# Gated encoder block on one core: the order of PSUM readings and attention-row sums around the gate products

## The chip, the cores and the metric

The kernel runs on one core of a Trainium2 chip. The metric is the device time of one execution in microseconds (us); the time before is the median of three runs. The engines are TensorE (PE in the profile; PEld is its loading of weights), VectorE (DVE), ScalarE (ACT), GpSimd (POOL) and SyncE (SP), which issues the transfers (DMA).

## What is computed

One residual layer over 1024 tokens of width 1024, in float32. Cut to what matters here:

```
h    = rms_norm(x)
proj = h @ w_in            # q, k, v of two attentions, and the gates g_a, g_b (1024 columns each)
o_a  = neighbourhood_attention(...)    # 1024 x 512
o_b  = sliding_window_attention(...)   # 1024 x 512
y    = sigmoid(g_a) * (o_a @ w_branch_a) + sigmoid(g_b) * (o_b @ w_branch_b)
x    = x + y @ w_out
x    = x + (silu(h2 @ w_gate) * (h2 @ w_up)) @ w_down      # h2 = rms_norm(x)
```

The change lies in the computation of g_a and g_b, and in the reading back of o_a and o_b, which the kernel has parked in DRAM.

## The kernel before

Every float32 operand is kept as two parts, hi (a cast, on ACT) and lo (the difference, on DVE). A product of a block is three matmuls of 128x512: hi by hi, hi by lo, lo by hi (L824 to L826).

The gates are computed in pairs. Pair d takes columns d of g_a and of g_b and both halves of the tokens, a product of 2 by 2 blocks, with seven block products instead of eight (class `Seven`, L788). Product p needs the weight g_p (hi and lo; some are sums s1 to s4 of weight blocks, made on DVE, L806), and one product is four blocks of three matmuls, twelve in all. The products of a pair run in the order (1, 5, 6, 2, 7, 3, 4) and add up in four PSUM banks named X, Y, V and Z; there are two such sets of banks, and pairs alternate between them. Pairs 2 and 3 are "early" (`early=d < 4`): they run in turn, product by product, in the order `EARLY` = (1, 2, 3, 5, 6, 7, 4), and there Z takes products 6, 7 and 4 on top of a copy of product 1. In the later pairs product 6 goes into Y, which begins as a copy of X, and ACT copies Y into Z (L828) before products 7 and 4 are added to it. The seventh pair is pair 7, the sixth pair 6.

A bank Z is read between products that go on adding to it: after product 6 in the early pairs (L889: Z plus the copy of V in `gp`), after product 7 (L893), and at the end (L875 in `out`). The next product into Z waits for such a reading. `out` (L874) multiplies a finished block by the row norms in `wide_rs` (into a tile `go`) and stores it in `g_dram`.

`load_o` (L919) reads back four rows (128 features each) of one attention output for one half of the tokens, each as two parts from `o_dram`; DVE adds the parts (L925, into one of two scratch tiles `os`), and `split` casts (ACT, L50) and subtracts (DVE, L51). Rows 4 to 7 belong to the sliding-window attention, rows 0 to 3 to the other. They are used after the gates, by the branch products (L427 to L429), which add into banks `pb`.

What sets the order: PE's is that of the program. SP's transfers made with `dma` (L95) keep the program's order too. On DVE and ACT a scheduler puts the instructions in order when the kernel is built, from its own estimate of times; `tc.issue_after(ins)` demands that what is made inside comes behind `ins` on that instruction's engine, and nothing else. Each engine then runs its queue in order. `prefetch(d + 2)`, behind product 2 in pairs 4 to 6, loads the weights of a later pair, or, from pair 6 on, the branch weights `wb` (`load_branch`, L931). Their casts and those of the next pair's weights are chained one behind the other (`in_chain`, L780).

## Time and profile before

| | |
|---|---|
| median of three runs | 1317.98 us (1316.93, 1317.98, 1318.95) |
| span of the profiled execution (first to last instruction) | 1314.8 us |
| what lies around the span, by the median | 3.2 us |
| mean granted TensorE clock | 1.000 |
| PE, DVE, ACT busy | 1304.5, 1018.5, 695.8 us |
| pairs 2 and 3 in the span | about 400.9 to 440.2 us |
| pairs 4 to 7 in the span | about 440.2 to 517.0 us |

The page shows the span of the profiled execution and no other time of it, so what lies around the span is taken from the median of the runs. Times in the timelines count from the span's start. A timeline row gives the start, the duration, the engine, the line, the operation, out<-in, the shapes, and in brackets the idle time of the engine before it and what ended that. Names are shown without buffer numbers, so `bankZ` stands for both banks Z and `go` for the tiles of all pairs. Lines are those of the kernel before.

### The profile page before, as it was taken

The numbers are of one execution on the slowest core, as the hardware profiler recorded it, in microseconds if no ns is written. First come the engines' busy times: TensorE is split into PE (matmuls) and PEld (weight loads), VectorE is DVE, ScalarE is ACT, GpSimd is POOL, SyncE is SP. The second block draws the span as 40 slices with busy tenths as digits, with TensorE's granted clock in tenths as the row PEclk, the third lists the DMA queues.
The fourth block names the chain that finished last, engine by engine and source line by source line (L and its number), as shares of the span: only waits on it lengthen the run. The fifth ranks groups of instructions, "written<-read, shape, count | busy, mean of one in ns | idle before, by whom it ended". The sixth has DMA issues, their size and how long they took to land.

```text
span 1314.8 us, 19624 instructions
## 1 busy us (share of the span) xinstructions
PE 1304.5 (99%) x6618; PEld 1133.6 (86%) x6618; DVE 1018.5 (77%) x2039; ACT 695.8 (53%) x1459; POOL 182.5 (14%) x322
## 2 busy tenths in 40 slices
PE   9999999999999999999999999999999999999998
PEld 8999999999888788888888888888888888888887
DVE  5678867776687758868999878888777799798774
ACT  6677857776664324636456544443444455363532
POOL 1364645564310000000000000000000000000000
PEclk9999999999999999999999999999999999999999
DMA  9532424252435348757774533233233356672532
GB/s 306 153 89 61 108 64 109 61 135 61 143 118 180 121 146 271 240 172 237 241 247 120 169 105 106 87 104 117 81 108 121 120 171 217 245 248 65 183 129 81
DMA packets 180997, 191.92 MB, mean 146 GB/s; under 512 B 21104, under 2 KB 126576, under 8 KB 180896
## 3 DMA queue, kind: packets, MB, share of 16 engines
q1 hardware_dynamic: 180640, 190.57, 46.5%
q8 instruction: 52, 0.85, 0.3%
q14 instruction: 49, 0.40, 0.1%
q10 hardware_dynamic: 256, 0.10, 0.0%
HBM read 133.19 MB, written 52.37 MB: 141 GB/s over the span
## 4 chain that ended last, share of the span: by engine, by line
PE 85%; DVE 6%; DMA 4%; ACT 2%; issue 1%; SPq 1%; POOL 1%; ACTq 0%; POOLq 0%; DVEq 0%
PE bankZ L824 6%; PE bankZ L825 5%; PE bankZ L826 5%; PE bankY L824 5%; PE bankY L826 5%; PE bankY L825 5%; PE pj L327 4%; PE bankX L824 4%; PE pj L326 4%; PE pj L325 4%; PE bankX L825 4%; PE bankX L826 4%; PE o L649 3%; PE bankV L825 3%; PE bankV L824 3%; PE bankV L826 3%
## 5 line engine op out<-in xcount | busy, mean ns | idle before, releaser
L603 ACT ACTIVATE E<-E,nm 128x384 f32<-128x384 f32 (+3 forms) x128 | 75.7, 592 | 48.3 <-DVE nm L597 42.4
L605 POOL TENSOR_SCALAR E<-E,nm 128x384 f32<-128x384 f32 (+1 forms) x128 | 74.3, 581 | 95.2 <-DVE nm L604 72.3
L51 DVE TENSOR_TENSOR pl<-tp,ph 128x384 fp32r<-128x384 f32 (+1 forms) x128 | 66.4, 519 | 17.2 <-ACT ph L50 16.2
L50 ACT CAST ph<-tp 128x384 fp32r<-128x384 f32 (+1 forms) x128 | 57.4, 449 | 20.5 <-PE tp L615 19.9
L50 ACT CAST f<-f 128x512 fp32r<-128x512 f32 x87 | 50.9, 620 | 22.2 <-DMA f<-u_dram 21.5
L51 DVE TENSOR_TENSOR f<-f 128x512 fp32r<-128x512 f32 x87 | 56.4, 684 | 8.0 <-ACT f L50 8.0
L615 PE MATMUL tp<-ident,E 128*128 128x128 f32 x352 | 59.5, 272 | 0.9 <-POOL E L605 0.9
L615 PEld LDWEIGHTS tp<-ident,E 128*128 128x128 f32 x352 | 45.2, 140 | 5.9 <-POOL E L605 1.2
L345 POOL TENSOR_TENSOR ss<-ss,mhalf 128x4 f32<-128x4 f32 (+2 forms) x42 | 49.7, 1184 | 3.2
L649 PE MATMUL o<-pl,v 128*128 128x256 f32 (+2 forms) x160 | 48.7, 305 | 0.6 <-DVE pl L51 0.5
L604 DVE RECIPROCAL nm<-nm 128x1 f32<-128x1 f32 x128 | 20.4, 160 | 36.1 <-ACT E L603 34.8
L1214 POOL TENSOR_TENSOR rs<-rs,mhalf 128x4 f32<-128x4 f32 x2 | 2.8, 1418 | 319.4 <-DVE rs L1213 319.4
L649 PE MATMUL o<-ph,v 128*128 128x256 f32 (+2 forms) x160 | 45.9, 301 | 0.5 <-ACT ph L50 0.5
L591 PE MATMUL s<-k,q 128*128 128x384 f32 (+1 forms) x128 | 46.0, 359 | 0.0
L592 PE MATMUL s<-k,q 128*128 128x384 f32 (+1 forms) x128 | 41.4, 323 | 0.0
L597 DVE CUSTOM_DVE_ANT_0 E<-s,bsw,cols 128x384 f32<-128x384 f32 (+1 forms) x64 | 37.0, 577 | 4.5 <-PE s L592 3.8
L1231 ACT ACTIVATE u<-u 128x512 f32<-128x512 f32 x44 | 27.5, 629 | 19.7 <-DVE u L1230 19.7
L597 DVE CUSTOM_DVE_ANT_0 E<-s,bna 128x384 f32<-128x384 f32 (+1 forms) x64 | 32.9, 517 | 4.2 <-PE s L592 3.7
L1232 DVE TENSOR_TENSOR u<-u,wide_rs 128x512 f32<-128x512 f32 x44 | 30.0, 687 | 6.4 <-ACT u L1231 5.6
L50 ACT CAST f_5h<-s1f 128x512 fp32r<-128x512 f32 x22 | 13.7, 622 | 39.5 <-DVE s1f L806 32.2
L824 PE MATMUL bankY<-f,f_6h 128*128 128x512 f32 x88 | 34.5, 392 | 0.1
L825 PE MATMUL bankV<-f,f_5h 128*128 128x512 f32 x88 | 34.4, 391 | 0.0
(1268 smaller groups left out, 4658.9 us busy)
## 6 DMA issues: line engine op xcount, KB each, us to landing
f<-u_dram SPq DMA_DIRECT2D x77, 256.0 KB
wg_s<-in_w_gate_dram SPq DMA_DIRECT2D x22, 512.0 KB
u_dram<-u SPq DMA_DIRECT2D x33, 256.0 KB
o_dram<-of SPq DMA_DIRECT2D x32, 256.0 KB
o<-o_dram SPq DMA_DIRECT2D x32, 256.0 KB
sg<-g_dram SPq DMA_DIRECT2D x32, 256.0 KB
g_dram<-go SPq DMA_DIRECT2D x24, 256.0 KB
u_dram<-tau SPq DMA_DIRECT2D x22, 256.0 KB
```

The lines of the kernel that those rows point to most:

```text
L50: a = nc.scalar.copy(hi, src)
L51: b = (eng or nc.vector).tensor_tensor(lo, src, f(hi), ALU.subtract)
L325: nc.tensor.matmul(ps[:, :384], lh, his[k][:, :384], start=(k == 0), stop=False)
L326: nc.tensor.matmul(ps[:, :384], lh, los[k][:, :384], start=False, stop=False)
L597: att["bound"] = nc.vector.tensor_tensor_reduce(E[:, :n], s[:, :n], hd["bias"](qb), -1.0, sk if sw else 1e30, ALU.add, ALU.min, nm[:, 0:1] ...
L603: nc.scalar.activation(E[:, :m], E[:, :m], AF.Exp, bias=nm[:, 0:1], scale=-1.0, accum_out=nm[:, 1:2])
L605: nc.gpsimd.tensor_scalar(E[:, :n], E[:, :n], nm[:, 1:2], 1.0, op0=ALU.mult, op1=ALU.mult)
L615: nc.tensor.transpose(tp[:, tok(j)], hd["E"][qq][:, ko:ko + P], ident)
L649: nc.tensor.matmul(hd["O"][half][:, (a - half * 4) * P:(z + 1 - half * 4) * P], v[:, kb].rearrange("p a e -> p (a e)"), pp[:, (a - q0) * P ...
L824: nc.tensor.matmul(ps, hi[:, tok(j)], bh, start=first, stop=False, skip_group_check=True)
L825: nc.tensor.matmul(ps, hi[:, tok(j)], bl, start=False, stop=False, skip_group_check=True)
L826: nc.tensor.matmul(ps, lo[:, tok(j)], bh, start=False, stop=end, skip_group_check=True)
```

## The change

It moves instructions and adds or removes none. In the early pairs, the reading of Z after product 6 stays where it is in the program, but the second sum (with Y) and the scalings of both high halves move behind product 4, with an `issue_after` on the last reading of Z that was made (`att["z"]`). Since the two pairs run in turn, that is the third pair's reading after product 7, for both of them. In `load_o`, the sums and casts of the rows are taken out into `split_o`; for the rows loaded behind the fifth pair they come behind product 6 of the sixth pair, with an `issue_after` on the copy of Y into Z. The other three row groups are loaded first (all eight transfers) and then summed, at the same places in the program.

```diff
@@ gate_pair
             elif p == 6 and s.early:
-                nc.vector.tensor_add(ga[:, HI], z, p5[:, LO])
-                nc.vector.tensor_add(ga[:, HI], y, ga[:, HI])
-                out(0, 1, ga[:, HI], ga[:, HI])
+                att["z"] = nc.vector.tensor_add(ga[:, HI], z, p5[:, LO]).ins
             elif p == 7:
-                nc.vector.tensor_add(p5[:, HI], z, p5[:, LO])
-                out(1, 1, gb[:, HI], p5[:, HI])
+                att["z"] = nc.vector.tensor_add(p5[:, HI], z, p5[:, LO]).ins
+                if not s.early:
+                    out(1, 1, gb[:, HI], p5[:, HI])
             elif p == 3 and not s.early:
...
             elif p == 4:
+                if s.early:
+                    with tc.issue_after(att["z"]):
+                        nc.vector.tensor_add(ga[:, HI], y, ga[:, HI])
+                        out(0, 1, ga[:, HI], ga[:, HI])
+                        out(1, 1, gb[:, HI], p5[:, HI])
                 out(1, 0, gb[:, LO], z)
@@ load_o
                 dma(f(z), o_dram[tok(8 * part + r), half_cols(half)])
+
+    def split_o(r0, half):
+        for r in range(r0, r0 + 4):
+            hi, lo = o_rows[r, half]
             both = scratch(f"os{r}_{half}")
             nc.vector.tensor_tensor(both, f(hi), f(lo), ALU.add)
             split(hi, lo, both)
+
+    def rows_o(r0, half):
+        load_o(r0, half)
+        split_o(r0, half)
+
+    def behind_copy():
+        with tc.issue_after(pairs[6].copied):
+            split_o(4, 0)
@@ the loops
     for d in range(4, 7):
-        run(gates(d, ORDER, {4: lambda: load_o(4, 0)} if d == 5 else {}))
+        run(gates(d, ORDER, {5: {4: lambda: load_o(4, 0)}, 6: {6: behind_copy}}.get(d, {})))
 
     def behind_two():
         load_branch(1)
-        load_o(4, 1)
-
-    run(gate_pair(7, ORDER, {1: lambda: load_sg(0, 0), 6: lambda: load_o(0, 0), 2: behind_two, 3: lambda: load_o(0, 1)}))
+        rows_o(4, 1)
+
+    run(gate_pair(7, ORDER, {1: lambda: load_sg(0, 0), 6: lambda: rows_o(0, 0), 2: behind_two, 3: lambda: rows_o(0, 1)}))
```

In the queues this moves the following. First DVE, in the early pairs, from the second pair's reading of Z after product 6 on; `go_0_5707`, `gp_5709`, `bankZ_5553` and `bankY_5551` are the second pair's, `go_0_5723`, `gp_5725`, `bankZ_5557` and `bankY_5555` the third's, and the rows on `g_` and `s2g` to `s4g` prepare the fourth pair's weights. Before:

```order
L889 TENSOR_TENSOR go_0_5707<-bankZ_5553,gp_5709 128x512
L51 TENSOR_TENSOR g_5l<-s1g_5812,g_5h 128x512
L806 TENSOR_TENSOR s2g_5813<-ga4s,s1g_5812 128x512
L890 TENSOR_TENSOR go_0_5707<-bankY_5551,go_0_5707 128x512
L875 TENSOR_TENSOR go_0_5707<-go_0_5707,wide_rs_111 128x512
L889 TENSOR_TENSOR go_0_5723<-bankZ_5557,gp_5725 128x512
L51 TENSOR_TENSOR g_6l<-s2g_5813,g_6h 128x512
L51 TENSOR_TENSOR g_2l<-ga4s,g_2h 128x512
L806 TENSOR_TENSOR s3g_5814<-gb_5809,ga4s 128x512
L890 TENSOR_TENSOR go_0_5723<-bankY_5555,go_0_5723 128x512
L893 TENSOR_TENSOR gp_5709<-bankZ_5553,gp_5709 128x512
L875 TENSOR_TENSOR go_0_5723<-go_0_5723,wide_rs_111 128x512
```

The same place in the changed kernel, where L889, L891 and L900 are the lines of the two readings of Z and of the sum with Y:

```order
L889 TENSOR_TENSOR go_0_5707<-bankZ_5553,gp_5709 128x512
L51 TENSOR_TENSOR g_5l<-s1g_5812,g_5h 128x512
L806 TENSOR_TENSOR s2g_5813<-ga4s,s1g_5812 128x512
L889 TENSOR_TENSOR go_0_5723<-bankZ_5557,gp_5725 128x512
L51 TENSOR_TENSOR g_6l<-s2g_5813,g_6h 128x512
L51 TENSOR_TENSOR g_2l<-ga4s,g_2h 128x512
L806 TENSOR_TENSOR s3g_5814<-gb_5809,ga4s 128x512
L891 TENSOR_TENSOR gp_5709<-bankZ_5553,gp_5709 128x512
L51 TENSOR_TENSOR g_7l<-s3g_5814,g_7h 128x512
L806 TENSOR_TENSOR s4g_5815<-ga4s,s2g_5813 128x512
L891 TENSOR_TENSOR gp_5725<-bankZ_5557,gp_5725 128x512
L900 TENSOR_TENSOR go_0_5707<-bankY_5551,go_0_5707 128x512
```

All four readings of a bank Z (two of each pair) now stand ahead of the sums with Y and of the scalings.

Next ACT in the sixth pair (`bankX_5550` to `bankZ_5553`, and `gp_6267`, which is `gp_6251` in the changed kernel), from its copy of X into Y to the casts of the branch weights. Before:

```order
L828 COPY bankY_5551<-bankX_5550 128x512
L50 CAST o_0_6237<-os_0_6240 128x512
L887 COPY gp_6267<-bankV_5552 128x512
L50 CAST o_0_6244<-os_0_6247 128x512
L50 CAST o_0_6251<-os_0_6254 128x512
L828 COPY bankZ_5553<-bankY_5551 128x512
L50 CAST o_0_6258<-os_0_6261 128x512
L50 CAST wb10h<-wb0s 128x512
```

And changed:

```order
L828 COPY bankY_5551<-bankX_5550 128x512
L887 COPY gp_6251<-bankV_5552 128x512
L828 COPY bankZ_5553<-bankY_5551 128x512
L50 CAST o_0_6237<-os_0_6323 128x512
L50 CAST o_0_6240<-os_0_6327 128x512
L50 CAST o_0_6243<-os_0_6331 128x512
L50 CAST o_0_6246<-os_0_6335 128x512
L50 CAST wb10h<-wb0s 128x512
```

The copy into Z has moved ahead of the three row casts that stood before it.

Last DVE in the sixth pair, from the sum of the first row (`os_0` from `o_0`) to the subtraction of the fourth; `go_0_6265` and `go_0_6249` are the sixth pair's. Before:

```order
L925 TENSOR_TENSOR os_0_6240<-o_0_6237 128x512
L51 TENSOR_TENSOR o_0_6237<-os_0_6240,o_0_6237 128x512
L925 TENSOR_TENSOR os_0_6247<-o_0_6244 128x512
L925 TENSOR_TENSOR os_0_6254<-o_0_6251 128x512
L51 TENSOR_TENSOR o_0_6244<-os_0_6247,o_0_6244 128x512
L51 TENSOR_TENSOR o_0_6251<-os_0_6254,o_0_6251 128x512
L925 TENSOR_TENSOR os_0_6261<-o_0_6258 128x512
L875 TENSOR_TENSOR go_0_6265<-bankX_5550,wide_rs_110 128x512
L51 TENSOR_TENSOR o_0_6258<-os_0_6261,o_0_6258 128x512
```

And changed, where L933 is the line of the sum:

```order
L933 TENSOR_TENSOR os_0_6323<-o_0_6237 128x512
L933 TENSOR_TENSOR os_0_6327<-o_0_6240 128x512
L51 TENSOR_TENSOR o_0_6237<-os_0_6323,o_0_6237 128x512
L51 TENSOR_TENSOR o_0_6240<-os_0_6327,o_0_6240 128x512
L933 TENSOR_TENSOR os_0_6331<-o_0_6243 128x512
L933 TENSOR_TENSOR os_0_6335<-o_0_6246 128x512
L875 TENSOR_TENSOR go_0_6249<-bankX_5550,wide_rs_110 128x512
L51 TENSOR_TENSOR o_0_6243<-os_0_6331,o_0_6243 128x512
L51 TENSOR_TENSOR o_0_6246<-os_0_6335,o_0_6246 128x512
```

The scaling of bank X still stands behind all four sums, now with two of the subtractions behind it instead of one. In the seventh pair the scaling of bank X comes ahead of the first row sum, which it followed; the rest of the differences there are of the same kind, and behind the second of the four branch stages all queues are as before. PE's queue is the same throughout, and SP's differs only in the order of the stores of pairs 2 and 3.

## The prediction

> **What bounds the kernel now.** I read the page first: the length of the execution, the busy times, and the chain of work that ended last.

> ```profile
> span 1314.8 us, 19624 instructions
> PE 1304.5 (99%) x6618; PEld 1133.6 (86%) x6618; DVE 1018.5 (77%) x2039; ACT 695.8 (53%) x1459; POOL 182.5 (14%) x322
> ...
> PE 85%; DVE 6%; DMA 4%; ACT 2%; issue 1%; SPq 1%; POOL 1%; ACTq 0%; POOLq 0%; DVEq 0%
> ```

> TensorE (PE) is busy for 1304.5 of 1314.8 us and makes up 85% of the last chain. A change on VectorE (DVE) or ScalarE (ACT) therefore pays only where PE stands still. The list of waits, for PE over the whole run, tells where that is in the gates:

> ```profile
> PE bankZ L824 <- ACT bankZ L828: 0.4, 1, 0.4
> PE bankZ L824 <- DVE go L889: 0.3, 1, 0.3
> ```

> Two waits, both for a PSUM bank Z. A wait shorter than the modelled end of the product before it does not show as idle time, so I went on to the starts of the products in the timeline. Undisturbed, they start 0.23 us apart and twelve (one of a pair's seven products) take 440.15 to 442.87, which is 2.72 us:

> ```profile
> 428.08 0.39 PE L824 MATMUL bankZ<-hs,g_7h 128*128 128x512 f32 x1
> ...
> 430.60 0.39 PE L826 MATMUL bankZ<-hs,g_7l 128*128 128x512 f32 x1
> 431.30 0.47 PE L824 MATMUL bankZ<-hs,g_7h 128*128 128x512 f32 x1 [0.31 <-DVE go L889]
> ...
> 433.91 0.39 PE L826 MATMUL bankZ<-hs,g_7l 128*128 128x512 f32 x1
> 434.30 0.47 PE L824 MATMUL bankZ<-hs,g_4h 128*128 128x512 f32 x1
> ...
> 436.90 0.39 PE L826 MATMUL bankZ<-hs,g_4l 128*128 128x512 f32 x1
> 437.31 0.47 PE L824 MATMUL bankZ<-hs,g_4h 128*128 128x512 f32 x1
> ...
> 440.15 0.39 PE L824 MATMUL bankX<-h,g_1h 128*128 128x512 f32 x1
> ...
> 442.87 0.39 PE L824 MATMUL bankV<-hs,g_5h 128*128 128x512 f32 x1
> ```

> Three steps are longer than 0.23 us: 0.70, 0.39 and 0.41. DVE's timeline says what each waited for:

> ```profile
> 429.14 0.68 DVE L890 TENSOR_TENSOR go<-bankY,go 128x512 f32<-128x512 f32 x1
> ...
> 430.47 0.68 DVE L889 TENSOR_TENSOR go<-bankZ,gp 128x512 f32<-128x512 f32 x1
> ...
> 433.47 0.68 DVE L893 TENSOR_TENSOR gp<-bankZ,gp 128x512 f32<-128x512 f32 x1
> ...
> 436.48 0.68 DVE L893 TENSOR_TENSOR gp<-bankZ,gp 128x512 f32<-128x512 f32 x1
> ```

> The three readings of a bank Z end at 431.15, 434.15 and 437.16, and PE goes on 0.15 us after each. The second place is in the sixth pair:

> ```profile
> 486.39 0.39 PE L824 MATMUL bankX<-h,g_2h 128*128 128x512 f32 x1
> ...
> 488.88 0.39 PE L826 MATMUL bankX<-h,g_2l 128*128 128x512 f32 x1
> 489.69 0.50 PE L824 MATMUL bankZ<-hs,g_7h 128*128 128x512 f32 x1 [0.41 <-ACT bankZ L828]
> ...
> 497.98 0.39 PE L824 MATMUL bankX<-h,g_1h 128*128 128x512 f32 x1
> 487.80 0.69 DVE L925 TENSOR_TENSOR os<-o 128x512 f32<-128x512 f32 x1 [0.68 <-DMA o<-o_dram]
> 488.53 0.62 ACT L50 CAST o<-os 128x512 fp32r<-128x512 f32 x1 [0.75 <-DVE os L925]
> 489.05 0.58 ACT L828 COPY bankZ<-bankY 128x512 f32<-128x512 f32 x1
> ```

> PE had finished product 6 before 486.39, so the copy of Y into Z could have run then. On ACT it stood behind a cast whose sum waited for a loaded row.

> **The change, part by part.** No instruction comes or goes; the work is put in another order.

> *Pairs two and three.* From 428.08 to 440.15 PE issues 48 products in 12.07 us; at 2.72 us for twelve they need 10.88. **1.19 us** are lost, of which 0.81 are the three long steps (0.47 + 0.16 + 0.18). In the new order the third pair's L889 stands where L890 ran, so it ends at about 429.8; PE needs its bank at 428.08 + 2.72 = 430.80. The second pair's reading of product 7 stands three rows later, at about 431.7 once product 7 has ended near 431.0, and is over by 432.4 (needed at 433.52). The third pair's follows two rows (one with a cast between) later, near 433.8 to 434.4, needed at 436.24. All three have 1 us or more to spare, so I take the whole 1.19 us; between nothing and that lies this term. What is moved back, two sums and four scalings, delays no one: the Y bank is next written a pair later, and the stores of the scaled rows now stand in another order on SP, where nothing but stores follows until the load of the sixth pair's weights:

> ```profile
> 452.36 0.39 SPq L97 DMA_DIRECT2D ga6s<-in_w_in_dram  x1
> ```

> The last row of the group reads bank Z once PE's last product of the two pairs has ended, which is about 440.15, and takes 0.68, so this load has some 11 us of cover; with the cover gone, each row moved ahead of it would cost its 0.68 us.

> *Sixth pair.* From 486.39 to 497.98 there are again 48 products, in 11.59 us: **0.71 us** are lost. With the copy ahead of the four casts it runs when product 6 is done, two products ahead of its use. I take all 0.71.

> That is 1.90 us at 497.98, where the seventh pair begins. Whether it lasts depends on what stands ready there:

> ```profile
> 490.39 0.69 DVE L875 TENSOR_TENSOR go<-bankX,wide_rs 128x512 f32<-128x512 f32 x1
> ...
> 497.08 0.68 DVE L51 TENSOR_TENSOR g_1l<-ga7s,g_1h 128x512 fp32r<-128x512 f32 x1
> 491.51 0.39 SPq L97 DMA_DIRECT2D wb0s<-in_w_branch_b_dram  x1
> 494.39 0.62 ACT L50 CAST wb10h<-wb0s 128x512 fp32r<-128x512 f32 x1 [3.27 <-DMA wb0s<-in_w_branch_b_dram]
> ```

> The seventh pair's low weight g_1l is ready at 497.76 and used by the third product, at 498.44: 0.68 us to spare. It hangs on a chain that PE does not drive directly: the scaling of bank X at 490.39, its store, behind it on SP the load of the branch weights at 491.51, their casts from 494.39, and only then the seventh pair's. If PE comes 1.90 us earlier, this chain must come 1.22 earlier. Its start is behind the four row sums. The rows' loads are issued after the fifth pair's last store and so come 1.19 earlier: the third sum, which ran at 487.80 as its row landed, becomes possible at 486.6, the first two before it. Product 6's last matmul starts 0.23 before 486.39 and takes 0.39, so it ends at 486.55, and now 1.19 earlier: the copy takes ACT from about 485.4 to 486.0. Two casts follow to 487.1, their subtractions end at 487.9, the third and fourth sum run from 487.8 and 488.4, and the scaling starts at 489.0 instead of 490.39: 1.4 earlier, enough by 0.2. Were the first two sums also held until the copy ends, it would start at 489.8, and PE would lose 0.6. I take nothing lost and keep 0.6 as the end of the range.

> ```profile
> 532.89 0.39 PE L428 MATMUL pb<-o,wb00h 128*128 128x512 f32 x1
> 531.34 0.68 DVE L51 TENSOR_TENSOR o<-os,o 128x512 fp32r<-128x512 f32 x1
> ...
> 509.06 0.69 DVE L875 TENSOR_TENSOR go<-bankX,wide_rs 128x512 f32<-128x512 f32 x1 [0.97 <-PE bankX L826]
> 510.00:520.00 10.00, 10.00 (x46) 8.28 (x45) 9.82 (x17) 3.90 (x8) 0.00 (x0) 1.00 0.90 271
> ```

> The next tight place is the last attention row: low part ready at 532.02, read at 532.89. It must come 1.03 earlier. DVE is busy for 9.82 of the 10 us from 510 (third busy time of the row), after a scaling at 509.06 that PE releases, so it begins 1.9 earlier, with one sum (0.60) more behind that point: 1.3 earlier. Enough; if not, up to 1.0 is lost.

> ```profile
> 585.28 0.32 SPq L97 DMA_DIRECT2D y_dram<-tby  x1
> 604.73 0.62 ACT L50 CAST o_1h<-wo_0s 128x512 fp32r<-128x512 f32 x1 [2.99 <-DMA wo_0s<-in_w_out_dram]
> 609.10 0.58 ACT L828 COPY bankY<-bankX 128x512 f32<-128x512 f32 x1
> 609.73 0.50 PE L824 MATMUL bankX<-y,o_2h 128*128 128x512 f32 x1
> ```

> At 609.73 PE has no margin at all: it starts 0.05 us after a copy that stands behind casts of loaded weights. A stretch of transfers that begins with the store at 585.28 decides it. That store waits for a sum (tby) of the third of four branch stages, hence for PE's products, so I let the stretch move along and lose nothing; the other end is the whole 1.90.

> [...] The granted clock of the slices with the stops:

> ```profile
> 430.00:440.00 10.00, 9.67 (x41) 7.08 (x40) 9.56 (x16) 2.32 (x4) 0.00 (x0) 1.00 0.29 109
> 480.00:490.00 10.00, 9.59 (x42) 7.63 (x42) 4.20 (x7) 3.41 (x6) 0.00 (x0) 1.00 0.75 235
> ```

> It is 1.00, and products after a stop start 0.23 us apart again from the second on. [...]

> **The sum**: 1.19 + 0.71 = 1.90 us off a span of 1314.8, so 1312.9. The median of the runs shown is 3.2 us above the span; leaving that as it is, 1317.98 − 1.90 = **1316.1 us**, 0.14% faster.

> **Rivals.**
> - *Part of it is lost again* on one of the three tight places (0.6, 1.0 or all of 1.90): 1316.7 to 1318.0. For it: margins of 0.2, 0.3 and none. Against: each chain begins with something that PE releases. Chance 0.18.
> - *It does not do what it says in the sixth pair*: the copy comes early, but the weights behind the branch loads then hold PE for the same 0.71. 1316.8; chance 0.07.
> - *Slower*: the four rows go one at a time through sum, cast and subtraction (0.69 + 0.62 + 0.69 = 2.0 us each), begun only after the copy at 486.0. The scaling of bank X then starts at 494.0, 5.0 late against 489.0, and every microsecond beyond the 0.2 of margin goes to PE: 4.8 − 1.9 = 2.9 us slower, 1320.9. It turns into a loss once the scaling starts after 491.1. Against: two scratch tiles, and two sums stand ahead of the first subtraction. Chance 0.06.
> - *The stops also cost clock*: if the twelve products after each of the four stops ran at half speed, each stop would give back another 2.72 us: 1317.98 − 1.90 − 10.9 = 1305.2. The granted clock of 1.00 and the 0.23 us speak against it. Chance 0.02.

> **How the numbers follow.** The forecast has 0.67. What a measurement of this kernel can tell from no change is about 0.2%, 2.64 us, and the forecast is below that; the runs shown differ by 2.0 us, so 0.15 of the forecast's share may be read as faster. Faster: 0.15 + 0.02 = 0.17. Slower: 0.06. The same: 0.77. For the range, the low end is the forecast less the scatter (1317.98 − 1316.93 = 1.05, and 0.3 if the stop at 609.73 goes too): 1314.7. The high end is all of it lost and two thirds of the upper scatter (0.97): 1318.6.

> **What would show it.** Right: no step above 0.3 us between the product starts of pairs two and three, the copy of Y into Z straight after the sixth pair's product 6, the scaling of bank X about 1.4 us earlier, no new wait at the seventh pair's third product, at the last attention row or around 608. Wrong: a PE wait for g_1l or for a row's low part, or a stop near 608 that has grown by the gain.

## The result, and the profile after

| comparison | changed, median (runs) | before, median (runs) | ratio, 95% interval |
|---|---|---|---|
| first | 1314.91 us (10; 1313.71 to 1317.18) | 1317.68 us (10; 1315.54 to 1319.57) | 0.9981 (0.9973 to 0.9989) |
| second | 1315.76 us (11; 1313.58 to 1320.47) | 1316.30 us (33; 1314.65 to 1320.09) | 0.9995 (0.9984 to 1.0006) |
| third | 1314.72 us (11) | 1316.19 us (29) | 0.9988 (0.9980 to 0.9997) |

The first comparison is the result; the other two came with the experiments below. The predicted 1316.1 lies 1.2 us above the first median, inside the range of 1314.7 to 1318.6. Over the three comparisons the mean of the 32 runs of the changed kernel is 1315.25 us and that of 71 runs of the kernel before 1316.72: 1.48 us less, with a 95% interval of about 0.9 to 2.1 (twice a standard error of 0.30). So the change is a small gain of some 0.11%. Single executions above 2000 us, of which the third comparison has one among its 29, are in no mean. The gain is not one of clock: among the runs of the second and third comparison with a mean clock of 1.000, the kernel before has a mean of 1316.21 (48 runs) and the changed kernel one of 1314.93 (18), 1.28 less.

The page of the first profile of the changed kernel, its length, its busy times and the chain of work that ended last:

```profile
span 1315.2 us, 19621 instructions
...
PE 1304.1 (99%) x6618; PEld 1134.0 (86%) x6618; DVE 1018.6 (77%) x2039; ACT 695.5 (53%) x1459; POOL 182.8 (14%) x322
...
PE 84%; DMA 7%; DVE 5%; ACT 2%; issue 1%; SPq 1%; POOL 1%; POOLq 0%; ACTq 0%; DVEq 0%
```

Nothing here tells a gain: the span is 0.4 us longer than before. This execution took 1317.18 us, the longest of the ten. What the change did has to be read where it stands. Pairs 2 and 3 on PE, and the three readings of a bank Z on DVE:

```profile
427.62 0.39 PE L824 MATMUL bankZ<-hs,g_7h 128*128 128x512 f32 x1
...
430.34 0.39 PE L824 MATMUL bankZ<-hs,g_7h 128*128 128x512 f32 x1
...
433.06 0.39 PE L824 MATMUL bankZ<-hs,g_4h 128*128 128x512 f32 x1
...
435.78 0.39 PE L824 MATMUL bankZ<-hs,g_4h 128*128 128x512 f32 x1
...
438.50 0.39 PE L824 MATMUL bankX<-h,g_1h 128*128 128x512 f32 x1
428.49 0.68 DVE L889 TENSOR_TENSOR go<-bankZ,gp 128x512 f32<-128x512 f32 x1
...
431.13 0.68 DVE L891 TENSOR_TENSOR gp<-bankZ,gp 128x512 f32<-128x512 f32 x1
...
433.26 0.69 DVE L891 TENSOR_TENSOR gp<-bankZ,gp 128x512 f32<-128x512 f32 x1
```

Four products of twelve take 2.72 us each, 10.88 together instead of 12.07. The readings end at 429.17, 431.81 and 433.95, and PE needs them at 430.34, 433.06 and 435.78.

The sixth pair, and behind it the seventh, with the chain to its g_1l (PE, ACT, DVE and SP, each in order of time):

```profile
484.74 0.39 PE L824 MATMUL bankX<-h,g_2h 128*128 128x512 f32 x1
...
487.46 0.39 PE L824 MATMUL bankZ<-hs,g_7h 128*128 128x512 f32 x1
...
495.84 0.39 PE L825 MATMUL bankX<-h,g_1h 128*128 128x512 f32 x1
496.27 0.50 PE L826 MATMUL bankX<-h,g_1l 128*128 128x512 f32 x1
496.61 0.40 PE L824 MATMUL bankX<-h,g_1h 128*128 128x512 f32 x1
484.94 0.57 ACT L828 COPY bankZ<-bankY 128x512 f32<-128x512 f32 x1 [2.13 <-PE bankY L826]
...
493.07 0.62 ACT L50 CAST wb10h<-wb0s 128x512 fp32r<-128x512 f32 x1 [3.84 <-DMA wb0s<-in_w_branch_b_dram]
488.49 0.68 DVE L875 TENSOR_TENSOR go<-bankX,wide_rs 128x512 f32<-128x512 f32 x1
...
495.53 0.69 DVE L51 TENSOR_TENSOR g_1l<-ga7s,g_1h 128x512 fp32r<-128x512 f32 x1
489.61 0.39 SPq L97 DMA_DIRECT2D wb0s<-in_w_branch_b_dram  x1
```

The copy into Z is done at 485.51, 1.95 us ahead of its use (one product ahead, and not two as the prediction has it), and product 7 follows product 2 after 2.72 us: the stop is gone. But at 496.27 PE waits for g_1l (ready at 496.22): this step is 0.43 and the next 0.34 instead of 0.23, 0.3 us lost.

Further on, the two places where the gain went in this execution. First the start of the output pairs, then the opening of the feed-forward part (`f_7h` is the weight of its product 7; the sixteen products of one column are the sums of the row norm; `s1f` is a DVE sum on the weights loaded last):

```profile
607.52 0.58 ACT L828 COPY bankY<-bankX 128x512 f32<-128x512 f32 x1
608.16 0.50 PE L824 MATMUL bankX<-y,o_2h 128*128 128x512 f32 x1 [0.39 <-ACT bankY L828]
678.16 0.69 DVE L806 TENSOR_TENSOR s1f<-wu__7961 128x512 f32<-128x512 f32 x1 [1.44 <-DMA wu__7961<-in_w_up_dram]
697.63 0.58 ACT L828 COPY bankZ<-bankY 128x512 f32<-128x512 f32 x1
695.60 1.84 PE L1227 MATMUL bankV<-ones,wide_rs 128*128 128x1 f32 x16
698.26 0.80 PE L824 MATMUL bankZ<-f,f_7h 128*128 128x512 f32 x1 [0.82 <-ACT bankZ L828]
```

And the same stretch by windows (busy times of PE, PEld, DVE, ACT and POOL, then the granted clock, the share of the DMA engines and GB/s), in the kernel before and in the changed one:

```profile
698.00:702.00 4.00, 3.96 (x22) 3.36 (x22) 4.00 (x8) 4.00 (x8) 0.00 (x0) 1.00 0.16 59
```

```profile
698.00:702.00 4.00, 3.73 (x11) 2.99 (x11) 4.00 (x9) 4.00 (x8) 0.50 (x1) 0.61 0.01 4
```

PE waits 0.82 us for a copy of Y into Z on ACT. In the 4 us it issues 11 products of 512 columns, where the kernel before issued 13 in the 3 us from 699.01 (the other nine of its 22 are the last of the small ones): the granted clock is 0.61, and the products behind the stop start 0.43 us apart instead of 0.23. The copy stands at the end of a chain on DVE and ACT that begins with a loaded weight and has no gap: from `s1f` at 678.16 to the copy at 697.63 it takes 19.47 us, as before (19.48, from 678.90 to 698.38).

The difference to the profile of the kernel before, at the same product of the program, named by its time before (minus is earlier):

| at | first profile | second | third | pairs 2 and 3 alone | rows alone |
|---|---|---|---|---|---|
| 428 | −0.46 | +0.06 | +0.20 | +0.40 | +0.55 |
| 440 | −1.65 | −1.13 | −0.99 | −0.79 | +0.09 |
| 490 | −2.34 | −1.82 | −1.68 | −0.58 | −0.60 |
| 499 | −2.05 | −1.56 | −1.52 | −0.59 | −0.63 |
| 609 | −1.89 | −1.55 | −1.48 | −0.59 | −0.63 |
| 660 | −1.44 | −2.04 | −1.65 | −0.53 | −0.87 |
| 707 | +0.01 | −2.86 | −2.45 | −0.86 | −1.70 |
| end | +0.31 | −2.31 | −2.80 | −1.02 | −1.61 |

The first line is scatter: up to 428 the queues of all these kernels are the same. Between 428 and 499 the changed kernel gains 1.59, 1.62 and 1.72 us in its three profiles, against this one profile of the kernel before. The ninth and the twelfth run below have the queues of the kernel before up to 695, and their profiles are 0.49 and 0.62 us shorter between 428 and 499 than this one. Against the mean of the three the changed kernel gains 1.2 to 1.4 us there. Behind 600 the lines go either way, by up to 2 us.

### The profile page after: what moved, and what is told of

It is laid out like the page before. It is cut to its first block, busy times and chain, and to the rows that moved or that the text cites. A ratio compares the mean times of both kernels' runs of the same rounds, so it can differ in the third digit from the quotient of the medians.

```text
span 1315.2 us, 19621 instructions
## 1 busy us (share of the span) xinstructions
PE 1304.1 (99%) x6618; PEld 1134.0 (86%) x6618; DVE 1018.6 (77%) x2039; ACT 695.5 (53%) x1459; POOL 182.8 (14%) x322
## 4 chain that ended last, share of the span: by engine, by line
PE 84%; DMA 7%; DVE 5%; ACT 2%; issue 1%; SPq 1%; POOL 1%; POOLq 0%; ACTq 0%; DVEq 0%
PE bankZ L824 5%; PE bankZ L825 5%; PE bankZ L826 5%; PE bankY L824 5%; PE bankY L825 5%; PE bankY L826 5%; PE bankX L826 4%; PE bankX L824 4%; PE bankX L825 4%; PE pj L326 4%; PE pj L325 4%; PE pj L327 4%; PE o L649 3%; PE bankV L825 3%; PE bankV L824 3%; PE bankV L826 3%
## 5 line engine op out<-in xcount | busy, mean ns | idle before, releaser
L51 DVE TENSOR_TENSOR pl<-tp,ph 128x384 fp32r<-128x384 f32 (+1 forms) x128 | 66.4, 519 | 17.2 <-ACT ph L50 16.1
L50 ACT CAST ph<-tp 128x384 fp32r<-128x384 f32 (+1 forms) x128 | 57.4, 449 | 20.4 <-PE tp L615 19.9
L50 ACT CAST f<-f 128x512 fp32r<-128x512 f32 x87 | 50.9, 620 | 25.5 <-DMA f<-u_dram 24.9
L51 DVE TENSOR_TENSOR f<-f 128x512 fp32r<-128x512 f32 x87 | 56.4, 683 | 8.3 <-ACT f L50 8.1
L824 PE MATMUL bankZ<-f,f_7h 128*128 128x512 f32 x88 | 35.0, 397 | 0.8 <-ACT bankZ L828 0.8
L826 PE MATMUL bankZ<-f,f_7l 128*128 128x512 f32 x88 | 34.7, 395 | 0.0
L825 PE MATMUL bankZ<-f,f_7h 128*128 128x512 f32 x88 | 34.7, 394 | 0.0
```

The source lines that it names most:

```text
L50: a = nc.scalar.copy(hi, src)
L51: b = (eng or nc.vector).tensor_tensor(lo, src, f(hi), ALU.subtract)
L824: nc.tensor.matmul(ps, hi[:, tok(j)], bh, start=first, stop=False, skip_group_check=True)
L825: nc.tensor.matmul(ps, hi[:, tok(j)], bl, start=False, stop=False, skip_group_check=True)
L826: nc.tensor.matmul(ps, lo[:, tok(j)], bh, start=False, stop=end, skip_group_check=True)
```

## The experiments

**The changed kernel twice more**, unaltered. The first time:

> The changed kernel once more, unaltered, for a second profile beside the kernel before on the same chip. In the first profile the gain is 2.2 us at the start of the seventh pair, 1.5 us at 660 and nothing at 707: TensorE stands still for 0.82 us before the first bank Z product of the feed-forward part (698.26), and then runs at a granted clock of 0.61 between 698 and 702. Theory A (the low clock is an accident of some executions): a mean clock of 1.000, products 0.23 us apart behind that stop, a span of 1312 to 1313.5, and 1 us or more of the gain left at 707; if the clock falls again, the span is 1314.5 to 1315.5. Theory B (the gain is always eaten there): span 1314.5 or more whatever the clock shows, and a median no more than 0.5 us below the kernel before. Median by A: 2 to 3 us below.

The second time, beside the ninth and tenth run:

> The changed kernel once more, unaltered, beside the two above. Theory A: a mean 0.9 to 1.6 us below the kernel before, low-clock runs in 1 or 2 of 11, and in the profile 1.2 us gained at 440, 0.7 at 489, 0.3 lost at 499. Rival: no difference in the mean by more than 0.5 us.

The second profile (span 1312.5):

```profile
676.04 0.68 DVE L806 TENSOR_TENSOR s1f<-wu__7961 128x512 f32<-128x512 f32 x1
695.52 0.58 ACT L828 COPY bankZ<-bankY 128x512 f32<-128x512 f32 x1
696.71 0.48 PE L824 MATMUL bankZ<-f,f_7h 128*128 128x512 f32 x1
```

and its window:

```profile
698.00:702.00 4.00, 4.00 (x19) 3.31 (x18) 4.00 (x9) 3.69 (x7) 2.62 (x2) 1.00 0.02 4
```

The load landed 2.1 us earlier, so `s1f` and, 19.48 us behind it, the copy came earlier by as much; PE found the bank ready, and the clock stayed at 1.00. So what the first profile lost at 698 belongs to that execution, as theory A had it; the medians of these two comparisons are 0.54 and 1.47 us below the kernel before, the means 0.91 and 1.53, where A asked for a median 2 to 3 below the first time. Of the third set's other figures the 1.2 and 0.7 us came out, while 0.2 instead of 0.3 us were lost at 499, and 3 of the 11 runs had a low clock, where 1 or 2 were expected. The load is the last of a stretch, from about 645 to 677, in which the DMA engines are busy nearly throughout in both kernels (a share of 0.99 before, 1.02 in the first profile of the changed kernel). In the eight profiles that have these queues there, `s1f` ran between 676.04 and 678.90; PE waited for the copy in four of the five in which it ran at 677.96 or later, and in none of the others.

**Each part alone.** Pairs 2 and 3 only (the first part of the diff), and the rows only (the two others):

> Pairs 2 and 3 as in the changed kernel, the attention rows as before. Theory A (the terms of the sum stand and add up): the three long steps between product starts are gone, 1.2 us gained at 440 (pairs 2 and 3 in 10.9 us instead of 12.07), the stop of 0.81 us ahead of the sixth pair's product 7 still there; 1 to 1.5 us below the kernel before at the end. Rival (the copy into Z behind the casts is late by the time of the loads, not of TensorE): that stop grows from 0.81 to about 2.0 us, and the gain at the seventh pair is nothing; the median is within 0.5 us of the kernel before.

> The attention rows as in the changed kernel, pairs 2 and 3 as before. Theory A: the sixth pair takes 10.9 us instead of 11.59, 0.7 us gained at the seventh pair, no wait for its g_1l; 0.5 to 1 us below the kernel before at the end. Rival (the seventh pair's weights or the last attention row take the 0.7 us back): a step of more than 0.3 us at the seventh pair's third product or at the last row of the first branch product, and a median within 0.3 us of the kernel before.

The last two columns of the table are theirs. Pairs 2 and 3 alone gain 1.19 us from 428 to 440, the same as in the whole change; the rows alone 0.69 from 440 to 490. (That they also gain 0.46 from 428 to 440, where nothing was changed, is the first of the three long steps, which this execution did not have: a DVE sum on a loaded weight, from which DVE works with hardly a gap up to the reading of Z (in the kernel before its instructions start 0.60 to 0.77 us apart from 426.55 to 430.47), began 1.99 us before the product at 428 and not 1.53, as its load had landed earlier.) The waits of PE in the first of the two still show the sixth pair's stop:

```profile
PE bankZ L824 <- ACT bankZ L828: 0.6, 1, 0.6
```

It is 1.01 between starts, where it was 0.81: the copy waits for a loaded row (DVE stands still for 0.81 us ahead of that row's sum, at 487.21). The rival asked for 1.2 us more and got 0.20, and that is within what the row's landing does by itself, since with the queues of the kernel before this step was 0.26 and 0.34 in the ninth and twelfth run. The medians, 1315.55 (0.9994, 0.9985 to 1.0003) and 1315.50 us (0.9993, 0.9984 to 1.0002), stand 0.75 and 0.80 below the kernel before's 1316.30; neither can be told from no change, nor from the whole change.

**Two rows behind the scaling of bank X** (`att["x"]`), to test the chain to g_1l; `behind_scaling` stands behind product 2 of the sixth pair:

```diff
     def behind_copy():
         with tc.issue_after(pairs[6].copied):
-            split_o(4, 0)
+            split_o(4, 0, 2)
+    def behind_scaling():
+        with tc.issue_after(att["x"]):
+            split_o(6, 0, 2)
+        prefetch(8)
```

> The changed kernel, with the sums and casts of the third and fourth attention row behind the sixth pair's scaling of bank X, which then stands behind two sums instead of four. In both profiles of the changed kernel the seventh pair's third product came late by 0.17 to 0.20 us and the next step was 0.34 instead of 0.23, 0.29 to 0.32 us together, because the casts of the branch weights began 3.43 to 3.46 us after the issue of their load against 2.88 before. Theory A (that chain, from the scaling over its store and the loads, holds the seventh pair's g_1l): the scaling and the load are issued about 1.2 us earlier against TensorE, the two long steps are 0.23 again, 0.3 us gained at 499; what follows is left alone. Rival (VectorE is the bound there, since the two sums only move behind the scaling): the step stays at 0.4 or grows. Median: 0 to 0.6 us below the changed kernel.

```profile
488.19 0.69 DVE L875 TENSOR_TENSOR go<-bankX,wide_rs 128x512 f32<-128x512 f32 x1 [0.29 <-PE bankX L826]
...
495.03 0.68 DVE L51 TENSOR_TENSOR g_1l<-ga7s,g_1h 128x512 fp32r<-128x512 f32 x1
496.37 0.39 PE L825 MATMUL bankX<-h,g_1h 128*128 128x512 f32 x1
496.60 0.39 PE L826 MATMUL bankX<-h,g_1l 128*128 128x512 f32 x1
496.83 0.39 PE L824 MATMUL bankX<-h,g_1h 128*128 128x512 f32 x1
```

The scaling now waits for PE itself (against the lead at 428 it came 0.8 us earlier than in the first profile, where 1.2 were expected), g_1l is ready 0.89 us before its use, and both steps are 0.23: theory A holds, and the 0.3 us are what that chain cost. The end shows nothing of it (1315.68 us, 0.9995, 0.9985 to 1.0005): in this profile the stop at 698 was 1.2 us, with a granted clock of 0.57 behind it.

**The output pairs' copy first.** The weights of product 5 and later are prepared behind the first pair's copy of X into Y (`first` holds the two pairs, each of which is run up to product 1):

```diff
     for p in FIRST:
         for i in range(2):
             pairs[i].prepare(p)
+        if p == 2:
+            for g in first:
+                next(g)
+            chain.append(pairs[0].copied)
-    in_turn(*(out_pair(i, ...) for i in range(2)))
+    in_turn(*first)
```

> The changed kernel, with the weights of product 5 and later of the first two output pairs prepared behind the first pair's copy of X into Y. In five profiles the step ahead of product 2 (607 to 610) was 0.78, 0.62, 0.58, 0.45 and 0.34 or less, never 0.23 in all of them, since the copy stands behind a cast whose VectorE sum follows casts of loaded weights. Theory A (that place takes between 0 and 0.55 us back, by when the load lands): the step is 0.23, and 0.2 to 0.5 us are gained at 612 that stay as far as 690. Rival (VectorE's chain from the loaded weights is the bound, and product 5 or the second pair's copy waits for the same time): a step of 0.5 us or more stands within the next 20 us. Median: 0 to 0.6 us below the changed kernel.

```profile
610.89 0.58 ACT L828 COPY bankY<-bankX 128x512 f32<-128x512 f32 x1
...
611.52 0.50 PE L824 MATMUL bankX<-y,o_2h 128*128 128x512 f32 x1 [0.17 <-ACT bankY L828]
```

The first pair's product 2 now follows after 0.23 us, but the second pair's copy has come behind three casts, and PE stops there instead, by 0.56 between starts: 0.49 us were lost from 610 to 625. That is the rival. 1315.52 us (0.9990, 0.9980 to 1.0000).

**The copies of Y into Z first, in the opening of the feed-forward part.** Two versions: one moves the row norm and its diagonals too (the fourth run), one the copies alone (the seventh; `both_blocks` is here product 6 of both pairs with its copies):

```diff
     add_up_ffn(4)
+    both_blocks()
     feed(*((3, j) for j in range(4)))
-    for i, g in enumerate((ga, gb)):
-        prepare_ffn((i, 3))
-        next(g)
+    prepare_ffn((0, 3), (1, 3))
```

> The changed kernel, and in the opening of the feed-forward part the two copies of Y into Z and the row norm ahead of the third group of row casts, and the diagonals of the norm ahead of the fourth. Theory A (the 0.82 us stop comes from the copy behind casts whose VectorE sums began with a landed load, and the low clock from that stop on top of sixteen products of one column): the stop is under 0.1 us, the clock 1.000 there, the first product 3 of the feed-forward part starts 1.5 to 2.5 us earlier than in the changed kernel, and the median is 0.5 to 2 us below the changed kernel's. Rival (VectorE, full from 678 to 707, is the bound): the stop moves to the diagonals or to product 3 with the same length, and the median is within 0.5 us of the changed kernel's. Second rival (the low clock comes from the products of one column alone): the clock falls although the stop is gone.

> The changed kernel, with only the two copies of Y into Z in the opening of the feed-forward part ahead of the third group of row casts; all other queues are as in the changed kernel. In four profiles the first bank Z product stood 1.88 to 2.66 us behind the last product of Y, of which 1.84 are sixteen products of one column. Theory A (the copy behind the casts makes the stop, and the low clock follows when the quiet stretch gets longer than some 2 us): the first bank Z product starts at most 0.1 us behind the sixteen, no low clock there, and fewer of the runs show a mean clock below 1.000 than the 2 in 10 and 1 in 11 of the changed kernel and the 7 in 33 of the kernel before; the wait moves to the diagonals of the norm, and the median is 0 to 0.7 us below the changed kernel. Rival (the runs with a low clock have it from elsewhere, as around 810 in the fourth run): as many runs with a low clock as before.

In the fourth run the stop at 698 was gone, and another came at 808, in the products of quarter blocks, where the scheduler had put DVE and ACT in a new order. The waits of PE:

```profile
PE bankY L824 <- ACT bankY L1341: 2.1, 1, 2.1
```

and the window behind it:

```profile
810.40:814.00 3.60, 3.54 (x9) 2.81 (x10) 1.79 (x3) 1.66 (x4) 0.00 (x0) 0.54 0.04 8
```

Against the kernel before it lost 2.3 us at that stop and 1.27 in the low clock behind it, and was slower: 1317.61 us (1.0010, 1.0001 to 1.0018). In the seventh run, whose other queues are unchanged, the first bank Z product came 1.70 us behind the first of the sixteen, with no wait, and the wait moved to the diagonals:

```profile
696.26 0.48 PE L824 MATMUL bankZ<-f,f_7h 128*128 128x512 f32 x1
...
702.63 0.60 PE L1241 MATMUL bankV<-dg,ones 128*128 128x128 f32 x3 [0.64 <-DVE dg L1236]
```

Its median is 1315.36 us (0.9991, 0.9981 to 1.0001). None of its 12 runs has a mean clock below 1.000, against 6 of 32 of the changed kernel and 24 of 107 of the kernel before (those runs whose clock is listed). With the three other sets below that have these copies first and the queues behind them unchanged, it is 2 of 45. Theory A holds for the clock; in the time nothing is gained, since PE now waits 0.64 us for DVE's diagonals.

**The same on the kernel before**, run twice:

> The kernel before, with only the two copies of Y into Z in the opening of the feed-forward part ahead of the third group of row casts, as in the seventh run. With that stop out of the way, the seventh run and this one differ by the change alone. Theory A (the change is worth 1.90 less 0.3 in the gates, and the scatter of the comparisons so far, from 0.5 to 2.8 us, comes from low-clock runs and the stretches behind loads): no or few low-clock runs here too, and a mean 1.0 to 1.9 us above the seventh run's 1315.40, so 1316.4 to 1317.3. Rival (TensorE only arrives earlier at a bound set by loads and VectorE behind 600, which eats the gain whatever the clock does): a mean within 0.6 us of 1315.4.

> The ninth run's kernel once more, since its mean of 1317.56 us was 0.3 above the expected 1316.4 to 1317.3 and above the kernel before, though only one of ten runs had a low clock; in its profile 3.0 us were lost in the first 20 us, of which 1.35 a wait for a loaded row and the rest a low clock behind it, and from 20 us to the end it was 1.26 us shorter than the profile of the kernel before. Theory A (the first 20 us, where everything waits for first loads, make the length of a run: an accident of each execution, no effect of the copies): a mean of 1316 to 1317 this time, and in the profile a time at 20 us within 1 us of the kernel before. Rival (the kernel with the copies first but without the change is slower by itself): a mean of 1317.2 or more again, and a loss in the profile that stands behind 600.

Means of 1317.56 and 1317.44 us, medians 1318.01 (1.0010, 1.0001 to 1.0019) and 1317.32 (1.0009, 0.9999 to 1.0018). Theory A missed twice: this kernel is about 1 us slower than the kernel before, and 2.1 slower than the same with the change (1315.40, the mean of the seventh run, on another chip, where the mean of the kernel before was 1316.66; here it was 1316.41 and 1316.33). Its loss does not stand behind 600 either, as the rival asked: the first profile had lost 2.2 us and the second 0.9 by 380, where all queues are those of the kernel before. In the first it was a wait of 1.35 us for ACT's row `h` (ACT was busy for 0.18 of the 2 us from 10, against 1.59 in the kernel before), and the clock. PE's row, and the windows around and behind it:

```profile
13.01 0.44 PE L325 MATMUL pj<-wg_2h,h 128*128 128x384 f32 x1 [1.35 <-ACT h L53]
```

```profile
11.00:14.42 3.42, 1.90 (x9) 1.26 (x8) 1.99 (x4) 2.16 (x4) 0.00 (x0) 1.00 1.03 336
14.42:17.83 3.41, 3.41 (x12) 3.41 (x12) 3.20 (x6) 3.01 (x6) 0.00 (x0) 0.50 0.93 313
```

Why two sets of runs agree on a microsecond that no changed instruction explains stays open. It bounds what can be said: a difference of 1 us between two kernels can come from a part that is the same in both.

**Longer stops**, to see what a stop costs in clock (the edit is shown in short: the other copies of that line stay single):

```diff
-                self.copied = nc.scalar.copy(Z, Y)
+                for _ in range({"g4": 6, "g5": 7, "g6": 9, "g7": 6}.get(self.nm, 1)):
+                    self.copied = nc.scalar.copy(Z, Y)
```

> The changed kernel, with the copy of Y into Z made 6, 7, 9 and 6 times (the last between other casts) in pairs 4 to 7, so that TensorE stands still ahead of product 7 by about 1.0, 1.5, 2.0 and 2.7 us. A cost of the clock is looked for: in the profiles so far a stop of 0.81 us left products 0.23 us apart, and one of 2.13 us was followed by six or more at 0.43. Theory A (a threshold between these): behind the shorter stops 0.23 from the second product on, behind those of 2 us and more seven to nine products at 0.43, 1.3 us lost on top of the stop. Rival (the clock falls because of the banks or the waits and not by the length): low clock behind every one, or behind none. The execution is longer by the sum of the stops, about 7 us, and 1.3 for each low stretch.

The first products behind the stops of pairs 4, 5 and 6, and for those of pairs 5 and 6 the window with the stop and the next:

```profile
451.70 0.50 PE L826 MATMUL bankZ<-hs,g_7h 128*128 128x512 f32 x1 [1.73 <-ACT bankZ L831]
...
473.31 0.50 PE L826 MATMUL bankZ<-hs,g_7h 128*128 128x512 f32 x1 [2.28 <-ACT bankZ L831]
...
495.40 0.62 PE L826 MATMUL bankZ<-hs,g_7h 128*128 128x512 f32 x1 [2.75 <-ACT bankZ L831]
```

```profile
471.73:475.15 3.42, 1.84 (x8) 1.54 (x9) 1.23 (x3) 1.46 (x3) 0.00 (x0) 1.00 0.69 200
475.15:478.56 3.41, 3.41 (x17) 2.83 (x16) 1.89 (x3) 0.63 (x1) 0.00 (x0) 1.00 0.71 190
492.21:495.63 3.42, 0.67 (x3) 0.24 (x3) 0.69 (x1) 3.26 (x7) 0.00 (x0) 1.00 0.37 116
495.63:499.04 3.41, 3.41 (x9) 2.63 (x9) 3.13 (x6) 2.88 (x6) 0.00 (x0) 0.50 0.38 114
```

The stops came out longer than meant, 1.73, 2.28, 2.75 and 4.17 us. Behind the first two the clock stays at 1.00; behind the others eight and some twelve products run 0.43 us apart. So theory A, with the edge between 2.28 and 2.75 here. It is no fixed length, though: 2.13 us at 808, 0.82 and 1.22 behind the sixteen products of one column in the first profile and the fifth run, and 1.35 in the opening of the ninth were enough. The last section shows what the drops have in common. This kernel was run once.

**Both additions together** (two rows behind the scaling, the copies first):

> The changed kernel with both additions that worked in their place: two attention rows behind the scaling of bank X, and the two copies of Y into Z ahead of the row casts in the opening of the feed-forward part. Theory A: no stop over 0.3 us at the seventh pair's third product, no low clock, a mean 0.3 to 0.8 us below the changed kernel's, and the interval of the ratio to the kernel before below 1 altogether. Rival (each is eaten by the stretch behind 600): a mean within 0.3 us of the changed kernel's.

No step over 0.23 us at the seventh pair's third product, no run with a low clock in eleven, and the shortest span of all profiles, 1311.8. But the mean, 1315.37 us, is within 0.3 of the changed kernel's 1315.25, and the ratio 0.9992 (0.9984 to 1.0001): the rival. No version was found that measurably beats the changed kernel.

## Why the prediction was right, and where it was off

**Pairs 2 and 3: 1.19 us.** Right: 1.19 in eight of the ten profiles that have the new order there, 1.14 in two. All three readings had more than a microsecond to spare, as the order of the queue gave it. The 1.19 us are the difference to one profile, though. The new order takes 10.88 us each time (10.93 in two), while the old order took 12.07, 12.11, 11.92 and 11.61 us in the four profiles that have it (the kernel before, the ninth, twelfth and third run), by when a load lands that DVE's chain begins with. Against the mean of these the gain is 1.05 us.

**The sixth pair: 0.71 us.** Right against the profile from which it was read: the 48 products take 10.88 us in all nine profiles with the rows moved and a single copy, and 11.59 there. But what the old order loses here depends on when the second row lands. In the ninth run, with the same queues, it landed half a microsecond earlier against PE, and so did what follows:

```profile
488.64 0.39 PE L824 MATMUL bankX<-h,g_2h 128*128 128x512 f32 x1
...
491.40 0.50 PE L824 MATMUL bankZ<-hs,g_7h 128*128 128x512 f32 x1
489.52 0.69 DVE L925 TENSOR_TENSOR os<-o 128x512 f32<-128x512 f32 x1 [0.70 <-DMA o<-o_dram]
```

The third sum comes 0.88 us behind the first product of g_2h, where it was 1.41, and product 7 follows after 2.76 us instead of 3.30. The 48 products took 11.07 us there, 11.12 in the twelfth run and 11.80 with pairs 2 and 3 alone, so that the old order loses 0.19 to 0.92 us. The 1.90 us of the sum are thus what one execution lost; with the queues of the kernel before, the other two profiles lost 1.42 and 1.28 in these two places. The prediction's chain of times held too. Taken 0.46 earlier for this execution's lead at 428, it had the copy into Z at 484.9, the end of the second cast at 486.6, the third sum at 487.3 and the scaling at 488.5; the profile has 484.94, 486.56, 487.29 and 488.49.

**The seventh pair's g_1l: nothing lost, 0.6 as the end.** Here it was off, by the 0.2 to 0.3 us that three profiles show. The scaling and the issue of the load came 1.4 us earlier against the lead, as said. The step that failed is the one that was not written down: that the load would take as long as before. From its issue (489.61) to the first cast (493.07) it took 3.46 us, against 2.88. It is 2.88 to 3.31 in the four profiles with the rows in their old order and 3.01 to 3.46 in the nine with the new one and a single copy. The margin left was 0.2, so that half a microsecond more had to show. Why the load takes longer is open: a store of a scaled row follows it more closely (2.2 us instead of 2.7), but in the tenth run that store came 3.5 us behind, and the load still took 3.41. In the forecast's own terms this was the rival "part of it is lost again", at half of its bound; 1.90 less 0.3 is 1.6, and the runs give 1.48, with an interval that holds 1.90 too.

**The last attention row: nothing lost.** Right, but for 0.14 us in the first profile.

**The start of the output pairs: moves along, nothing lost.** Right on the average only. The step at that place was 0.78, 0.23 and 0.42 in the three profiles of the changed kernel, 0.45 before, since the loads behind the store at 585 land by a few tenths earlier or later: from that store to the second cast into `o_1h` it is 19.45 us in the kernel before (585.28 to 604.73) and 19.78 in the first profile (583.38 to 603.16). "The other end is the whole 1.90" was too far: over all fourteen profiles the step is 0.81 at most, 0.58 more than undisturbed.

**What no term named** is the place at 698, and with it the largest effect in the first profile: 0.8 us of stop, 1.3 of low clock, the whole gain gone. Before, PE went on there 1.88 us behind the first of the sixteen small products, where 1.70 is the least: 0.18 us of wait already, which the list of waits didn't show, since those products count as busy for 1.84. A PE that comes 1.5 us earlier meets a copy behind a load that does not come earlier by as much (`s1f` ran 0.74 us earlier in the first profile). The prediction looked for such places up to 610 and not beyond.

**The clock.** The rival "the stops also cost clock" got 0.02, and at the four stops it was meant for that was right: they are gone, and no stretch of low clock went with them. But clock is lost to stops in this kernel at other places: to longer ones (2.13 us in the fourth run, 2.75 and 4.17 in the eighth), and to one of 0.82 us behind the sixteen small products.

**From the span to the time.** The 3.2 us around the span came from a median of three runs that was high: over 139 runs listed with their spans the difference is 1.98 us on the mean (1.7 to 2.5). The profile of before stands for 1316.8, and 1316.8 less 1.90 is 1314.9, the first median. So the 1.2 us between 1316.1 and 1314.9 are the base. That the first median then fits to the tenth is luck: in that comparison the two medians lie 2.77 us apart, more than the 1.90 that the change was to gain, and the mean of all 32 runs is 1315.25.

## What to carry to other kernels

When the engine that bounds a kernel gains a microsecond, follow its row to the very end and ask at each point that begins with a load whether that load moves along; a place where nothing waits today may only be covered by something small. Put the copy that an accumulation waits for ahead of work whose data come by DMA. And measure such an edit where it stands, by the starts of the same products, in several profiles of both kernels: the new order's 10.88 us were repeated there in eight of ten profiles, while the medians of three comparisons of the same two kernels differ by 0.5 to 2.8 us. A stop that hangs on a load has a different length in each execution (0.19 to 0.92 us in the sixth pair), so one profile of the kernel before does not price it.

## What was not expected of the hardware

What the drops have in common is how full the stretch before is. An estimate from the starts of the products counts each one for its columns at the full pace, 0.2275 us for 512. Leaving out the drop behind the last product, the six stretches ahead of a drop are then full to 9 to 39%, and of the stretches behind which the clock stayed, over 5,300 in the fourteen profiles, none is below 40%. This tells the 2.28 us that passed in one place from the 1.35 that did not in another: the stop of pair 5 lies across two stretches and leaves the second full to 50%, while that of the ninth run, with a second wait of 0.17 us, lies within one (39%). That the clock follows from this share is the author's reading of these profiles; no run varied it alone.

Sixteen products of one column, 1.84 us of PE "busy" time on the page, are next to nothing in this count (0.007 us). In the first profile of the changed kernel the clock fell at 697.75, only 0.31 us behind the end of the sixteen and before PE went on at 698.26, though the stretch that ended there shows PE busy for 3.12 of 3.42 us:

```profile
694.33:697.75 3.42, 3.12 (x23) 2.79 (x21) 3.42 (x7) 3.42 (x8) 0.00 (x0) 1.00 0.85 298
697.75:701.16 3.41, 2.90 (x7) 2.31 (x8) 3.41 (x6) 3.41 (x7) 0.00 (x0) 0.50 0.03 11
```

Counted by columns, this stretch is full to 37%. In the ten profiles without a wait behind the sixteen, no stretch there is full to less than 47%, and the clock stayed. They were not run alone.
